# A gated FFN in fp32 split products: two matmuls on the same weight block become one of 512 columns

## The chip, the cores and the metric

The kernel runs on one core of one Trainium2 chip (trn2). The metric is the device time of one execution in microseconds. Engines are named as in the profile: PE is the matmul engine and PEld its weight loads, DVE the vector engine, ACT the scalar engine, POOL the GpSimd engine; SPq and POOLq are the queues on which SyncE and GpSimd start transfers.

## The reference, cut to what matters

One layer of a hybrid block on 512 tokens of width 1024: two token mixers (gated linear attention and a forgetting attention), merged and projected, then a gated MLP of width 2816, then a norm. The change lies in the MLP:

```python
a, val = jnp.split(rmsnorm(x, norm_ffn_g) @ w_up, 2, axis=-1)
a = causal_dwconv(a, conv_w, conv_b)          # width 3, over the tokens
x = x + (jax.nn.gelu(a) * val) @ w_down
```

## The kernel before, in words

Every fp32 product is done as three products of parts: each operand is split into a high part and the rest (`wh`, `wl` of a weight piece, `xh`, `xl` of the activations), and `mm3` issues high-high, high-low and low-high into the same PSUM bank. In the FFN the weight is the stationary operand and the activations are what is streamed: the first matmul is `wh` with `ah`, the second `wh` with `al`, the third `wl` with `ah`, 256 columns each.

The up projection is done by a Strassen-like scheme with seven products instead of eight. The 22 feature tiles are taken as two plain ones (`NCL`) and `NSS` = 10 groups `g` of two. A group has seven products `p`, each with one weight piece of 128 x 1024 (a block of `w_up`, or a sum of blocks) and one operand `xops[p]` (a block of the activations, or a sum). One product is 2 feature tiles x 4 k-steps x 3 matmuls = 24 matmuls. I call the time of one product a slot. `SLOT` gives each product its place within its group; consecutive groups overlap, so that in steady state the order is, by slots of group g: 5(g), 7(g-1), 3(g), 4(g-1), 2(g), 6(g), 1(g+1), and again 5(g+1).

Three PSUM banks belong to a group: `x` gathers products 1 and 2, `z` gathers 5 and 3, `y` gathers 6, 7 and 4. After 1, 5 and 3 `joint` copies the bank to SBUF on ACT (L1461). After 6, DVE adds the copy of 1 onto the bank (L1505) and subtracts into `ap`; after 7 it subtracts again and the convolution follows: two ACT passes (L1393), four DVE multiply-adds (L1397), two Gelus (L1402). After 4 DVE multiplies `x` and `y` by the Gelus (L1520) into `act`, and `sums_of_acts` builds the operands of the down projection.

The weight pieces pass through three buffers (`NW`): `split_next` copies a raw piece to `wh` on ACT (L293) and subtracts to `wl` on DVE (L294), two slots ahead of its product. Behind the split, the `then` lists start what follows: the load of a later piece on SPq (L258), or the addition of a new block onto the raw piece just split, as a transfer with `accum_op=add` on POOLq (L301). These additions turn piece 5 into 6, 3 into 7 and 6 into 4. The piece of product 5 is itself a sum (k12 + k11); for groups 2 to 9 it is formed by `first_sum`: four POOL additions of 256 columns (L264), after the split of piece 2 of the group before.

The order on each engine is chosen by the framework's scheduler from the program order and its own estimates of durations, so it can differ a little from the order of the text.

Of the kernel before, what the change touches and what calls it, by code (L numbers as in the profile page):

```python
# [59 lines left out]
NCL = 2  # L60
NSS = (NF - NCL) // 2

SLOT = {1: -1, 5: 0, 3: 2, 2: 4, 6: 5, 7: 8, 4: 10}

EARLY = (6, 7)

# [24 lines left out]
def hybrid_kernel(ctx: ExitStack, tc, xT, xt, wp, wu, wd, wf, wn, pp, aw2, fing, out):  # L91
# [3 lines left out]
    cpool = ctx.enter_context(tc.tile_pool(name="cpool", bufs=1))  # L95
    wpool = ctx.enter_context(tc.tile_pool(name="wpool", bufs=1))
    banks_of = {}
    es_ps = [None]

    def psum(**tags):  # L100

        if es_ps[0] is not None:
            es_ps[0].close()
        es_ps[0] = ExitStack()
        for tag, bufs in tags.items():
            banks_of[tag] = es_ps[0].enter_context(
                tc.tile_pool(name="ps_" + tag, bufs=bufs, space=PSUM, reuse_waits="tile")
            )

# [6 lines left out]
    def pax():  # L116
        return bank("ax")

    ctx.callback(lambda: es_ps[0].close())
    psum(mm=4, ax=4)  # L120


# [92 lines left out]
    def behind(n, *what):  # L215
        then.setdefault(n, []).append(what)
# [10 lines left out]
    for g in range(NSS):  # L227
        for p, q in ((5, 6), (3, 7), (6, 4)):
            behind(at_step[g, p], "add", at_step[g, q])
        if g + 1 < NSS:  # L230
            if g > 0:
                behind(at_step[g, 2], "first sum", at_step[g + 1, 5], at_step[g + 1, 1])
            behind(at_step[g, 1], "load", at_step[g + 1, 1])
            behind(at_step[g, 2], "load", at_step[g + 1, 2])
        if g + 2 < NSS:
            behind(at_step[g, 7], "load", at_step[g + 2, 5])
            behind(at_step[g, 4], "load", at_step[g + 2, 3])
# [4 lines left out]
    for n, i in zip(freed, at_last):  # L242
        behind(n, "load", i)

    raws, splits, taken, first_copy, after_first, copied, added, last_load = {}, [], [0], [], [], [], [], []
    spare = {}
    rawx_pool, raw_pools = [], {"raw": wpool}

    def load_raw(n):
# [6 lines left out]
            raws[n] = rawx_pool[0].tile([P, 1024], F32, tag=place, name="rawx")  # L256
        for c in (slice(0, WF // 2), slice(WF // 2, WF)) if n == 0 else (slice(0, m),):
            last_load[:] = [nc.sync.dma_start(raws[n][:, c], new[:, c])]  # L258

    def first_sum(n, other, after):  # L260
        for i in range(4):
            c = slice(i * 256, (i + 1) * 256)
            with tc.issue_after(after.ins):
                nc.gpsimd.tensor_add(out=raws[n][:, c], in0=raws[n][:, c], in1=raws[other][:, c])  # L264

    def load_ahead(n):

# [4 lines left out]
    def split_next():  # L272
        n = len(splits)
        if n not in raws:
            load_raw(n)
        raw, m = raws[n], recipes[n][2]
        if n in spare:
            hi, lo = spare[n]()
        else:
            hi = wpool.tile([P, 1024], F32R, tag="wh", name="wh", bufs=NW)  # L280
            lo = wpool.tile([P, 1024], F32R, tag="wl", name="wl", bufs=NW)
        if n < KD:
            if n > 0:
                copied[:] = [nc.scalar.copy(out=hi[:, :WF], in_=raw)]
                copied.append(nc.vector.tensor_sub(out=lo[:, :WF], in0=raw, in1=hi[:, :WF].bitcast(F32)))
            else:
                a, b = slice(0, WF // 2), slice(WF // 2, WF)
                nc.vector.tensor_copy(out=hi[:, a], in_=raw[:, a])
                first_copy.append(nc.vector.tensor_sub(out=lo[:, a], in0=raw[:, a], in1=hi[:, a].bitcast(F32)))
                after_first.append(lambda: nc.scalar.copy(out=hi[:, b], in_=raw[:, b]))  # L290
                after_first.append(lambda: nc.vector.tensor_sub(out=lo[:, b], in0=raw[:, b], in1=hi[:, b].bitcast(F32)))
        else:
            nc.scalar.copy(out=hi[:, :m], in_=raw[:, :m])  # L293
            nc.vector.tensor_sub(out=lo[:, :m], in0=raw[:, :m], in1=hi[:, :m].bitcast(F32))  # L294
        splits.append((hi, lo))
        for what, i, *other in then.get(n, ()):
            if what == "load":
                load_raw(i)
            elif what == "add":
                raws[i] = raw  # L300
                added[:] = [nc.gpsimd.dma_start(raw, recipes[i][0], accum_op=ALU.add)]  # L301
            elif what == "sum":
                dma_behind(lo, raws[i], recipes[other[0]][0], accum_op=ALU.add)
            else:
                first_sum(i, *other, after=added[0])
        for i, b, c in adds_at.get(n, ()):
            dma_behind(lo, wsum[i][:, c], b[:, c], accum_op=ALU.add)

# [133 lines left out]

    xpool = ctx.enter_context(tc.tile_pool(name="xpool", bufs=1))

    xab = [xpool.tile([P, (KD - 2) * T], F32R, name=f"x{c}") for c in "hl"]
    xc = [xpool.tile([P, 1024], F32R, name=f"xc{i}") for i in range(2)]
    xh, xl = (
        [xab[i][:, k * T : (k + 1) * T] for k in range(KD - 2)] + [c[:, i * T : (i + 1) * T] for c in xc]
# [872 lines left out]
    with tc.issue_after(spread_rms(rt, rb).ins):  # L1321
# [8 lines left out]

    KH = KD // 2
    xo = npool.tile([P, 6 * KH * H], F32R, tag="xo", name="xo")
    places2 = [(xo[:, i * 2048 : i * 2048 + 1024], xo[:, i * 2048 + 1024 : (i + 1) * 2048]) for i in range(3)]
    places2 += [tuple(x[:, i * 1024 : (i + 1) * 1024] for x in xab) for i in range(3)] + [tuple(xc)]
    xops = {
        p: tuple(x.rearrange("p (k t) -> p k t", t=H) for x in pl) for p, pl in zip((1, 5, 3, 2, 6, 7, 4), places2)
    }
    x11, x12, x21, x22 = (xs[:, j * KH : (j + 1) * KH, i * H : (i + 1) * H] for i in range(2) for j in range(2))

    def split_x(p, src, after=None):  # L1340
# [63 lines left out]
    def halves(x):  # L1404
        return x.rearrange("p (i t) -> p i t", t=H)
# [40 lines left out]
    def up_product(ps, p, first):  # L1446

        wh, wl = piece()
        ah, al = xops[p]
        for i in range(2):  # L1450
            for k in range(KH):
                c = slice((i * KH + k) * P, (i * KH + k + 1) * P)

                mm3(
                    ps[:, i * H : (i + 1) * H], wh[:, c], wl[:, c], ah[:, k], al[:, k], first and i == k == 0,
                    k == KH - 1, skip_group_check=True,
                )

    def joint(ps):
        x = npool.tile([P, T], F32, tag="joint", name="joint", bufs=4)  # L1460
        nc.scalar.copy(out=x, in_=ps)  # L1461
        return x

    def down(ps, p, piece_no, ws, t2, c0=0, n=512, first=True):

        t = slice(t2 * P, (t2 + 1) * P)
        wh, wl = ws
        ah, al = ops[p % 2]
        for j in range(2):
            k = 2 * piece_no + j  # L1470
            if k == KB:
                break
            c = slice(j * 512 + c0, j * 512 + c0 + n)

            mm3(
                ps[:, c0 : c0 + n], ah[:, k, t], al[:, k, t], wh[:, c], wl[:, c], first and k == 0, k == KB - 1,
                skip_group_check=not first,
            )
# [2 lines left out]

    def first_down(i):
        if not acc1:
            acc1.extend((pax(), pax()))
        ws = piece()
        for t2 in range(2):
            down(acc1[t2], 0, i, ws, t2)

    st_of = {}
    for n, (g, p) in enumerate(steps):  # L1490
        for what in ahead_of.get(n, ()):
            what()
        st = st_of.setdefault(g, {})
        f = NCL + 2 * g
        name = {1: "x", 2: "x", 5: "z", 3: "z", 6: "y", 7: "y", 4: "y"}[p]
        first = name not in st
        if first:

            st[name] = (pax if name == "x" or g == 0 and name == "y" else pmm)()
        ps = st[name]  # L1500
        up_product(ps, p, first)
        if p in (1, 5, 3):
            st[p] = joint(ps)
        elif p == 6:
            nc.vector.tensor_add(out=ps, in0=ps, in1=st[1])  # L1505
            minus_sum(ap[:, :, 2 : H + 2], halves(ps), halves(st[3]))
        elif p == 7:
            minus_sum(ap[:, :, H + 2 : T + 2], halves(ps), halves(st[5]))
            t0 = st["t0"] = npool.tile([P, 2, T], F32, tag="t0", name="t0")
            for i in range(2):  # L1510
                convolve(f + i, i, t0)
        elif p == 4:
            t0 = st["t0"]
            if f // KB == (f + 1) // KB:
                parts = [(f // KB, slice(f % KB, f % KB + 2), slice(0, 2))]
            else:
                parts = [((f + i) // KB, slice((f + i) % KB, (f + i) % KB + 1), slice(i, i + 1)) for i in range(2)]
            for i, c in enumerate((st["x"], ps)):
                for j, k, fs in parts:
                    nc.vector.tensor_mul(  # L1520
                        out=act[j][:, i, k], in0=halves(c)[:, fs], in1=t0[:, fs, i * H : (i + 1) * H]
                    )
            for j, k, _ in parts:
                sums_of_acts(j, k)
        if g == NSS - 1 and p in EARLY:
            first_down(EARLY.index(p))
# [116 lines left out]
    product(2, acc1, first=False)  # L1643
    for t2 in range(2):
        add(acc1[t2], t2, 0, 1)
    acc3 = [pax(), pax()]
    product(3, acc3)
    for t2 in range(2):
        residual(acc3[t2], t2, 0, 512)
# [129 lines left out]
```

## Time and profile before

| | |
|---|---|
| median of 3 runs | 691.87 us (691.44 to 692.91) |
| the profiled execution | 691.86 us |
| its span, first to last instruction | 690.2 us |
| granted TensorE clock | 0.999 |
| busy over the span | PE 683.4, PEld 598.8, DVE 549.3, ACT 426.3, POOL 165.8 us |
| up projection by groups | about 376 to 573 us in the span |
| one period of seven slots in it | 20.16 us |

The shares of busy time say what is full on average; which engine sets the time of a stage is read from the spacing of its instructions and from the waits. A busy matmul is shown longer than the distance to the next one, because matmuls are pipelined; the distance between starts is what one costs in a stream.

### The profile page before, as it was taken

Reading aid. Unit: us, or ns where it says so; the run is one execution under the profiler, and the core shown is the slowest. Engines: PE = TensorE matmul, PEld = TensorE weight load, DVE = VectorE, ACT = ScalarE, POOL = GpSimd, SP = SyncE. Lnnn points to the kernel's source line nnn. Section 1 sums busy time; section 2 is a strip of 40 time slices with the busy share of each in tenths; the row PEclk is TensorE's granted clock in tenths of the full one; section 3 lists DMA queues with packets and bytes.
Section 4 is the critical chain, followed back from the end, with each engine's and each line's share of the span. In section 5 each row is a group of like instructions: output and inputs, shape, how many; then the busy total and the mean of one; then the engine's idle time right before and its main releaser. Section 6 shows DMA issues by size and latency. Waiting matters only on the chain.

```text
span 690.2 us, 11111 instructions
## 1 busy us (share of the span) xinstructions
PE 683.4 (99%) x4131; PEld 598.8 (87%) x4131; DVE 549.3 (80%) x831; ACT 426.3 (62%) x688; POOL 165.8 (24%) x212
## 2 busy tenths in 40 slices
PE   9999999999999999999999999999999999999996
PEld 6788888888888888888888999999999999888886
DVE  6774988858776766677689998888998889977984
ACT  7487676677777744334584866565555557655753
POOL 1125110123321424331110143332434410000222
PEclk9999999999999999999999999999999999999999
DMA  9769488989665489967974877887777788865643
GB/s 312 264 189 305 103 274 218 314 204 207 174 153 118 112 251 212 267 148 218 236 228 119 168 170 188 209 196 164 185 173 175 184 208 255 269 201 175 198 138 122
DMA packets 45034, 138.06 MB, mean 200 GB/s; under 512 B 5268, under 2 KB 9260, under 8 KB 44852
## 3 DMA queue, kind: packets, MB, share of 16 engines
q1 hardware_dynamic: 31156, 92.98, 39.6%
q0 software_dynamic: 10656, 39.33, 32.2%
q10 hardware_dynamic: 3168, 5.05, 2.0%
q8 instruction: 32, 0.52, 0.3%
q14 instruction: 22, 0.18, 0.1%
HBM read 133.13 MB, written 27.28 MB: 232 GB/s over the span
## 4 chain that ended last, share of the span: by engine, by line
PE 96%; DVE 2%; issue 0%; ACT 0%; ACTq 0%
PE ps_mm L330 22%; PE ps_mm L331 22%; PE ps_mm L332 22%; PE ps_ax L332 7%; PE ps_ax L331 7%; PE ps_ax L330 7%; PE ps_lg L1043 1%; PE ps_lg L984 1%; PE ps_pt L1018 1%; PE ps_mm L491 1%; DVE wl L294 1%; PE ps_ax L380 1%; PE ps_ax L887 1%; DVE xo L1344 1%; PE ps_ax L824 0%
## 5 line engine op out<-in xcount | busy, mean ns | idle before, releaser
L293 ACT CAST wh<-rawx 128x1024 fp32r<-128x1024 f32 x75 | 76.1, 1014 | 51.2 <-PE ps_mm L331 18.9
L330 PE MATMUL ps_mm<-xh,wh 128*128 128x512 f32 (+1 forms) x304 | 104.8, 345 | 0.0
L331 PE MATMUL ps_mm<-xl,wh 128*128 128x512 f32 (+1 forms) x304 | 103.2, 340 | 0.0
L332 PE MATMUL ps_mm<-xh,wl 128*128 128x512 f32 (+1 forms) x304 | 103.0, 339 | 0.0
L294 DVE TENSOR_TENSOR wl<-rawx,wh 128x1024 fp32r<-128x1024 f32 x75 | 89.8, 1203 | 14.1 <-ACT wh L293 14.0
L293 ACT CAST wh<-raw 128x1024 fp32r<-128x1024 f32 x58 | 60.6, 1046 | 36.1 <-PE ps_mm L331 30.8
L294 DVE TENSOR_TENSOR wl<-raw,wh 128x1024 fp32r<-128x1024 f32 x58 | 74.3, 1283 | 9.8 <-ACT wh L293 9.6
L330 PEld LDWEIGHTS ps_mm<-xh,wh 128*128 128x128 f32 x304 | 57.7, 190 | 7.6 <-issue 0.9
L332 PEld LDWEIGHTS ps_mm<-xh,wl 128*128 128x128 f32 x304 | 57.7, 190 | 6.5
L331 PEld LDWEIGHTS ps_mm<-xl,wh 128*128 128x128 f32 x304 | 57.7, 190 | 5.9 <-DVE xl L1253 0.2
L301 POOL DMA_DIRECT2D rawx<-in_wu_dram x30 | 26.1, 869 | 117.4 <-DVE wl L294 112.5
L294 DVE TENSOR_TENSOR wl<-rawz,wh 128x1024 fp32r<-128x1024 f32 x31 | 39.4, 1271 | 16.9 <-ACT wh L293 14.9
L264 POOL TENSOR_TENSOR rawx<-rawx,raw 128x256 f32<-128x256 f32 x32 | 39.1, 1250 | 27.2 <-DMA rawx<-in_wu_dram 27.2
L330 PE MATMUL ps_mm<-xo,wh 128*128 128x256 f32 x160 | 45.4, 284 | 0.0
L331 PE MATMUL ps_mm<-xo,wh 128*128 128x256 f32 x160 | 45.3, 283 | 0.0
L332 PE MATMUL ps_mm<-xo,wl 128*128 128x256 f32 x160 | 45.3, 283 | 0.0
L1397 DVE SCALAR_TENSOR_TENSOR t<-ap,ppt,t 128x512 f32<-128x512 f32 x44 | 44.9, 1072 | 0.0
L330 PE MATMUL ps_mm<-xc,wh 128*128 128x256 f32 (+1 forms) x128 | 42.8, 334 | 0.0
L331 PE MATMUL ps_mm<-xc,wh 128*128 128x256 f32 (+1 forms) x128 | 42.3, 330 | 0.0
L332 PE MATMUL ps_mm<-xc,wl 128*128 128x256 f32 (+1 forms) x128 | 42.2, 330 | 0.0
L293 ACT CAST wh<-rawz 128x1024 fp32r<-128x1024 f32 x31 | 32.4, 1044 | 14.1 <-issue 4.9
L330 PE MATMUL ps_mm<-wh,xh 128*128 128x512 f32 x96 | 37.7, 393 | 0.0
(487 smaller groups left out, 1967.4 us busy)
## 6 DMA issues: line engine op xcount, KB each, us to landing
rawx<-in_wu_dram POOLq DMA_DIRECT2D x32, 512.0 KB, 6.5
rawz<-in_wp_dram SPq DMA_DIRECT2D x30, 512.0 KB, 5.3
raw<-in_wp_dram SPq DMA_DIRECT2D x22, 512.0 KB, 4.9
wsum<-in_wd_dram SPq DMA_DIRECT2D x20, 512.0 KB, 6.6
rawx<-in_wu_dram SPq DMA_DIRECT2D x20, 512.0 KB, 6.2
raw<-in_wu_dram SPq DMA_DIRECT2D x20, 512.0 KB, 4.6
rawx<-wsum SPq DMA_DIRECT2D x12, 512.0 KB, 4.5
wsum<-in_wd_dram POOLq DMA_DIRECT2D x10, 512.0 KB, 8.1
```

Of the source, the lines that this page charges most:

```text
L264: nc.gpsimd.tensor_add(out=raws[n][:, c], in0=raws[n][:, c], in1=raws[other][:, c])
L293: nc.scalar.copy(out=hi[:, :m], in_=raw[:, :m])
L294: nc.vector.tensor_sub(out=lo[:, :m], in0=raw[:, :m], in1=hi[:, :m].bitcast(F32))
L301: added[:] = [nc.gpsimd.dma_start(raw, recipes[i][0], accum_op=ALU.add)]
L330: mm(ps, lhsT=ah, rhs=bh, start=start, stop=False, **k)
L331: mm(ps, lhsT=ah, rhs=bl, start=False, stop=False, **k)
L332: mm(ps, lhsT=al, rhs=bh, start=False, stop=stop, **k)
L380: mm(warm, lhsT=nc.const_aps.tensor(1.0, (P, P), BF16), rhs=nc.const_aps.tensor(1.0, (P, T), BF16), start=True, stop=True,)
L491: mm(first[i], lhsT=w[:, i * P : (i + 1) * P], rhs=x, start=(k == j == 0), stop=False)
L887: mm(obs[u][par][:, c], lhsT=scs[2 * u + par][:, 2 * t2 + j, :], rhs=vg[:, 2 * u + t2, h * GDV : (h + 1) * GDV], start=(t2 == j == 0), sto ...
L984: last = mm(lg[:, place_of_q(qb)], lhsT=a[r, q], rhs=b[r, :n], start=(j == 0), stop=(j == 2))
L1397: nc.vector.scalar_tensor_tensor(out=t0[:, i], in0=ap[:, i, w : w + T], scalar=col(C_CW + w * NF + f), in1=t0[:, i], op0=ALU.mult, op1=ALU ...
```

## The change

In groups 2 to 8 (`WIDE`), products 1, 5, 2 and 3 issue two matmuls for each feature tile and k-step instead of three. The first has `wh` as its weights and streams the 256 columns of `ah` and the 256 of `al` as one operand of 512 columns into one whole bank: the left half of the bank gathers high-high, the right half high-low. The second has `wl` and streams `ah` into the left half. So that both parts are reached by one access pattern, `xab` becomes one tile `xw`, and the operands are kept as `both[p]` = [128, 2, k, 256].

A wide tile takes two banks (one for each feature tile), and there are two wide tiles, which replace the four `ax` banks. The two halves are added on the way out: ACT copies the right halves to SBUF, DVE adds them to the left halves. This is done after each of the four products. After 1 the sum goes straight into the bank of `y`, in which 6, 7 and 4 then accumulate, so the DVE addition after 6 goes away in these groups; after 2 the sum goes into `act`, and the multiplication after 4 reads it there instead of in PSUM.

Products 2 and 3 change places in `SLOT`, in all groups. `first_sum` goes away: the sum k12 + k11 for groups 2 to 9 is made by an accumulating transfer on POOLq behind the split of piece 2, with a small POOL copy (`tick`) that holds it back until then. Groups 0, 1 and 9 keep the narrow products, with the evictions moved in the same way.

```diff
+WIDE = range(2, NSS - 1)
-SLOT = {1: -1, 5: 0, 3: 2, 2: 4, 6: 5, 7: 8, 4: 10}
+SLOT = {1: -1, 5: 0, 2: 2, 3: 4, 6: 5, 7: 8, 4: 10}
...
-                behind(at_step[g, 2], "first sum", at_step[g + 1, 5], at_step[g + 1, 1])
+                behind(at_step[g, 2], "sum", at_step[g + 1, 5], at_step[g + 1, 1])
...
-    def first_sum(n, other, after):
-        for i in range(4):
-            c = slice(i * 256, (i + 1) * 256)
-            with tc.issue_after(after.ins):
-                nc.gpsimd.tensor_add(out=raws[n][:, c], in0=raws[n][:, c], in1=raws[other][:, c])
...
-    xab = [xpool.tile([P, (KD - 2) * T], F32R, name=f"x{c}") for c in "hl"]
+    xw = xpool.tile([P, 2, (KD - 2) * T], F32R, name="xw")
+    xab = [xw[:, i] for i in range(2)]
...
+    def wide_product(ps, p, first):
+
+        wh, wl = piece()
+        for i in range(2):
+            for k in range(KH):
+                c = slice((i * KH + k) * P, (i * KH + k + 1) * P)
+                mm(ps[:, i], lhsT=wh[:, c], rhs=both[p][:, :, k], start=first and k == 0, stop=False, skip_group_check=True)
+                mm(
+                    ps[:, i, 0], lhsT=wl[:, c], rhs=both[p][:, 0, k], start=False, stop=k == KH - 1,
+                    skip_group_check=True,
+                )
+
+    def joint(g, ps, out=None, tag="joint3"):
+
+        if out is None or g in WIDE:
+            x = npool.tile([P, 2, H], F32, tag=tag, name=tag, bufs=2)
+            out = out or [(x, slice(0, 2))]
+        if g in WIDE:
+            nc.scalar.copy(out=x, in_=ps[:, :, 1])
+        for o, c in out:
+            if g in WIDE:
+                nc.vector.tensor_add(out=o, in0=ps[:, c, 0], in1=x[:, c])
+            else:
+                nc.scalar.copy(out=o, in_=halves(ps)[:, c])
+        return out[0][0]
...
+    psum(keep=1, wide=2)
...
-        up_product(ps, p, first)
-        if p in (1, 5, 3):
-            st[p] = joint(ps)
+        (wide_product if name != "y" and g in WIDE else up_product)(ps, p, first)
+        if p == 1 and g < WIDE[0]:
+            st[1] = joint(g, ps, [(act[1][:, 1, KB - 2 * g - 2 : KB - 2 * g], slice(0, 2))])
+        elif p == 1:
+            st["y"] = pmm()
+            joint(g, ps, [(halves(st["y"]), slice(0, 2))])
+        elif p == 2:
+            joint(g, ps, [(act[j][:, 0, k], fs) for j, k, fs in parts_of(f)])
+        elif p in (3, 5):
+            st[p] = joint(g, ps, tag=f"joint{p}")
         elif p == 6:
-            nc.vector.tensor_add(out=ps, in0=ps, in1=st[1])
-            minus_sum(ap[:, :, 2 : H + 2], halves(ps), halves(st[3]))
+            if g < WIDE[0]:
+                nc.vector.tensor_add(out=halves(ps), in0=halves(ps), in1=st[1])
+            minus_sum(ap[:, :, 2 : H + 2], halves(ps), st[3])
```

More of the change, by code (lines that the diff above doesn't have):

```diff
@@ L97, in hybrid_kernel, with psum @@
     banks_of = {}
[L98 to L104, printed above, removed]
+    es_ps = []
+    def psum(keep=0, **tags):
+        while len(es_ps) > keep:
+            es_ps.pop().close()
         for tag, bufs in tags.items():
-            banks_of[tag] = es_ps[0].enter_context(
+            es_ps.append(ExitStack())
+            banks_of[tag] = es_ps[-1].enter_context(
                 tc.tile_pool(name="ps_" + tag, bufs=bufs, space=PSUM, reuse_waits="tile")
@@ L117, in pax, with pwide @@
         return bank("ax")
-    ctx.callback(lambda: es_ps[0].close())
+    def pwide():
+        return banks_of["wide"].tile([P, 2, 512], F32, tag="wide", name="ps_wide")
+    ctx.callback(psum)
     psum(mm=4, ax=4)
@@ L243, in hybrid_kernel @@
         behind(n, "load", i)
-    raws, splits, taken, first_copy, after_first, copied, added, last_load = {}, [], [0], [], [], [], [], []
+    raws, splits, taken, first_copy, after_first, copied, last_load = {}, [], [0], [], [], [], []
     spare = {}
@@ L300, in split_next @@
                 raws[i] = raw
-                added[:] = [nc.gpsimd.dma_start(raw, recipes[i][0], accum_op=ALU.add)]
-            elif what == "sum":
+                nc.gpsimd.dma_start(raw, recipes[i][0], accum_op=ALU.add)
+            else:
                 dma_behind(lo, raws[i], recipes[other[0]][0], accum_op=ALU.add)
-            else:
-                first_sum(i, *other, after=added[0])
         for i, b, c in adds_at.get(n, ()):
@@ L1332, in hybrid_kernel @@
     xo = npool.tile([P, 6 * KH * H], F32R, tag="xo", name="xo")
[L1333 to L1337, printed above, removed]
+    places2 = [xo[:, i * 2048 : (i + 1) * 2048].rearrange("p (a n) -> p a n", a=2) for i in range(3)]
+    places2 += [xw[:, :, i * 1024 : (i + 1) * 1024] for i in range(3)]
+    both = {p: x.rearrange("p a (k t) -> p a k t", t=H) for p, x in zip((1, 5, 3, 2, 6, 7), places2)}
+    xops = {p: (x[:, 0], x[:, 1]) for p, x in both.items()}
+    xops[4] = tuple(x.rearrange("p (k t) -> p k t", t=H) for x in xc)
     x11, x12, x21, x22 = (xs[:, j * KH : (j + 1) * KH, i * H : (i + 1) * H] for i in range(2) for j in range(2))
@@ L1457, in up_product @@
                 )
[L1459 to L1462, printed above, removed]
+    def wide_product(ps, p, first):
[17 more added lines that the diff above has]
+                nc.vector.tensor_add(out=o, in0=ps[:, c, 0], in1=x[:, c])
+            else:
+                nc.scalar.copy(out=o, in_=halves(ps)[:, c])
+        return out[0][0]
     def down(ps, p, piece_no, ws, t2, c0=0, n=512, first=True):
@@ L1483, in first_down @@
         if not acc1:
-            acc1.extend((pax(), pax()))
+            acc = pwide()
+            acc1.extend(acc[:, t2] for t2 in range(2))
         ws = piece()
@@ L1487, in first_down, with parts_of @@
             down(acc1[t2], 0, i, ws, t2)
+    psum(keep=1, wide=2)
+    def parts_of(f):
+        if f // KB == (f + 1) // KB:
+            return [(f // KB, slice(f % KB, f % KB + 2), slice(0, 2))]
+        return [((f + i) // KB, slice((f + i) % KB, (f + i) % KB + 1), slice(i, i + 1)) for i in range(2)]
     st_of = {}
@@ L1497, in hybrid_kernel @@
         if first:
-            st[name] = (pax if name == "x" or g == 0 and name == "y" else pmm)()
-        ps = st[name]
-        up_product(ps, p, first)
-        if p in (1, 5, 3):
-            st[p] = joint(ps)
+            if name == "y":
+                st[name] = pmm()
+            elif g in WIDE:
+                st[name] = pwide().rearrange("p i (a t) -> p i a t", t=H)
+            else:
+                st[name] = pwide()[:, 0]
+        ps = st[name]
+        (wide_product if name != "y" and g in WIDE else up_product)(ps, p, first)
[8 more added lines that the diff above has]
+            st[p] = joint(g, ps, tag=f"joint{p}")
         elif p == 6:
-            nc.vector.tensor_add(out=ps, in0=ps, in1=st[1])
-            minus_sum(ap[:, :, 2 : H + 2], halves(ps), halves(st[3]))
+            if g < WIDE[0]:
+                nc.vector.tensor_add(out=halves(ps), in0=halves(ps), in1=st[1])
+            minus_sum(ap[:, :, 2 : H + 2], halves(ps), st[3])
         elif p == 7:
-            minus_sum(ap[:, :, H + 2 : T + 2], halves(ps), halves(st[5]))
+            minus_sum(ap[:, :, H + 2 : T + 2], halves(ps), st[5])
             t0 = st["t0"] = npool.tile([P, 2, T], F32, tag="t0", name="t0")
@@ L1513, in hybrid_kernel @@
             t0 = st["t0"]
[L1514 to L1519, printed above, removed]
+            for i in range(2):
+                for j, k, fs in parts_of(f):
+                    a = act[j][:, i, k]
                     nc.vector.tensor_mul(
-                        out=act[j][:, i, k], in0=halves(c)[:, fs], in1=t0[:, fs, i * H : (i + 1) * H]
+                        out=a, in0=a if i == 0 else halves(ps)[:, fs], in1=t0[:, fs, i * H : (i + 1) * H]
                     )
-            for j, k, _ in parts:
+            for j, k, _ in parts_of(f):
                 sums_of_acts(j, k)
@@ L1645, in hybrid_kernel @@
         add(acc1[t2], t2, 0, 1)
-    acc3 = [pax(), pax()]
+    acc = pwide()
+    acc3 = [acc[:, t2] for t2 in range(2)]
     product(3, acc3)
```

## The prediction, made before the changed kernel ran

> **What bounds the kernel now.** I read the page first, then the busy time by windows of one group period, then the distances between matmul starts, then each queue of one period.
>
> ```profile
> span 690.2 us, 11111 instructions
> PE 683.4 (99%) x4131; PEld 598.8 (87%) x4131; DVE 549.3 (80%) x831; ACT 426.3 (62%) x688; POOL 165.8 (24%) x212
> ...
> PE 96%; DVE 2%; issue 0%; ACT 0%; ACTq 0%
> ```
>
> The third line is the chain of work that ended last: 96% of it is PE. The next view is busy time by stretches of 20.16 us, one period of seven products (columns: PE, PEld, DVE, ACT, POOL, granted clock, DMA share, GB/s; the sum is over eight such stretches).
>
> ```profile
> 404.12:424.28 20.16, 20.16 (x170) 20.16 (x169) 18.10 (x21) 11.90 (x16) 7.21 (x8) 1.00 0.76 168
> 444.44:464.60 20.16, 20.16 (x170) 20.16 (x169) 17.20 (x19) 11.90 (x16) 7.58 (x8) 1.00 0.75 182
> 525.08:545.24 20.16, 20.16 (x170) 20.16 (x169) 17.80 (x19) 11.38 (x15) 8.02 (x9) 1.00 0.75 176
> sum 161.28, PE 161.28 PEld 161.28 DVE 140.45 ACT 93.41 POOL 57.53; mean PE 20.16 PEld 20.16 DVE 17.56 ACT 11.68 POOL 7.19
> ```
>
> PE has no gap, DVE is at 17.56 of 20.16 (87%), DMA at about 0.76. So in this stage a matmul less is time less, as long as nothing else reaches the period. What a matmul costs is the distance between starts. In the timeline of PE, the first of these rows and the last are 35 matmuls apart:
>
> ```profile
> 449.73 0.28 PE L330 MATMUL ps_mm<-xh,wh 128*128 128x256 f32 x1
> ...
> 453.93 0.28 PE L332 MATMUL ps_ax<-xo,wl 128*128 128x256 f32 x1
> ```
>
> (453.93 - 449.73) / 35 = 0.120 us for 256 columns; 168 of them are 20.16 us, the whole period. The 512-column matmuls of the down projection, 35 from the first to the second row below, and the two places where the width changes:
>
> ```profile
> 585.83 0.39 PE L330 MATMUL ps_ax<-wh,acth 128*128 128x512 f32 x1
> ...
> 593.76 0.39 PE L332 MATMUL ps_ax<-wh,actl 128*128 128x512 f32 x1
> ...
> 669.92 0.39 PE L332 MATMUL ps_ax<-wh,actl 128*128 128x512 f32 x1
> 670.15 0.28 PE L330 MATMUL ps_ax<-wh,acth 128*128 128x256 f32 x1
> 670.26 0.28 PE L331 MATMUL ps_ax<-wl,acth 128*128 128x256 f32 x1
> ...
> 671.58 0.40 PE L330 MATMUL ps_ax<-wh,acth 128*128 128x512 f32 x1
> 671.81 0.40 PE L331 MATMUL ps_ax<-wl,acth 128*128 128x512 f32 x1
> 672.05 0.39 PE L332 MATMUL ps_ax<-wh,actl 128*128 128x512 f32 x1
> 672.28 0.40 PE L330 MATMUL ps_ax<-wh,acth 128*128 128x512 f32 x1
> ```
>
> (593.76 - 585.83) / 35 = 0.2266 us. Doubling the columns adds 0.1066 us, so 0.0134 us of every matmul does not depend on its width.
>
> **The change, part by part.**
>
> *Matmuls.* Products 1, 5, 2, 3 in 7 groups, 8 pairs of feature tile and k-step each: 4 x 7 x 8 = 224 times, two matmuls of 0.120 become one of 0.2266: 0.0134 us saved, 3.0 us in all. The columns streamed stay the same; what goes is one start and one weight load. The unknowns are alternation and the access pattern. Narrow and wide now take turns; just after narrow ones, a 512 took (672.28 - 671.58) / 3 = 0.2333, which would halve the gain to 0.0067 each, 1.5 us; just after a wide one a 256 took 0.11, which speaks for the full gain. I take 0.0134, with 1.5 us as the low end. The wide operand is two runs of 256 columns apart in SBUF; no row before has that, and its bound is rival B.
>
> A page of the Trainium skill speaks against the 3.0. "TensorE: Matmul & The Clock Gate", section "Back-to-back issue gap", gives a gap of N / 2.4 + 2.5 ns at full clock, so a fixed part of 2.5 ns, by which 224 merges are worth about 0.6 us (an estimate). The rows here differ (13.4 ns beyond the same slope), and I go by the rows.
>
> *Evictions, DVE and ACT.* In each wide group DVE gains an addition after 1, 5, 3 and 2 and loses that after 6: three more. Each has one PSUM and one SBUF input, like L1505 (columns: busy us, mean ns):
>
> ```profile
> L1505 DVE TENSOR_TENSOR ps_mm<-ps_mm,joint 128x512 f32<-128x512 f32 x8 | 5.5, 689 | 0.0
> ```
>
> 3 x 0.69 = 2.1 us more per group. Against it stands what the POOL additions cost DVE today. The convolution's four multiply-adds in a group while POOL adds (422.8 to 427.5), and in the last group, where it does not (563 to 567):
>
> ```profile
> L1397 DVE SCALAR_TENSOR_TENSOR t<-ap,ppt,t 128x512 f32<-128x512 f32 x4 | 4.7, 1226 | 0.0
> ...
> L1397 DVE SCALAR_TENSOR_TENSOR t<-ap,ppt,t 128x512 f32<-128x512 f32 x4 | 2.7, 743 | 0.0
> ```
>
> With `first_sum` gone, 4 x (1.226 - 0.743) = 1.9 us per group come back. Net DVE is 17.56 + 2.1 - 1.9 = 17.8 of a new period of 20.16 - 32 x 0.0134 = 19.73 us (90%): hidden behind PE, cost 0. ACT gains one copy of the left-over half per group (0.58 us as the present `joint` copies have it, 11.7 to 12.3 of 19.73): 0. The place where DVE is latest is behind the convolution:
>
> ```profile
> 443.03 4.68 DVE L1397 SCALAR_TENSOR_TENSOR t<-ap,ppt,t 128x512 f32<-128x512 f32 x4
> 447.63 1.21 DVE L294 TENSOR_TENSOR wl<-rawx,wh 128x1024 fp32r<-128x1024 f32 x1
> ```
>
> This `wl` ends at 448.84 and its product begins at 449.37: 0.5 us to spare. Afterwards the convolution is 1.9 us shorter and one addition (after 2) comes in front: about 1.7 us to spare. If that cover were gone, lateness past 0.5 us would be PE time, rival C.
>
> *PSUM.* `x` and `z` rotate through two wide tiles. The next group's 5 needs `z` back two slots (5.6 us) after 3 ends; a copy (0.58) and an addition (0.69) fit. Cost 0; the exchange of 2 and 3 leaves 3 directly before 6, whose subtraction waits for the addition, still on DVE alone.
>
> *The sum of pieces as a transfer.* Per group, four POOL additions go; a `tick` copy, a POOLq issue (0.86 us) and 512 KB of accumulating DMA come, all for groups 2 to 9. Rows for 384 to 570 us (packets, MB, share of 16 engines; then count, size, us from issue to landing):
>
> ```profile
> q0 software_dynamic: 4035, 14.68, 48.7%
> q1 hardware_dynamic: 5328, 19.40, 28.3%
> ...
> rawx<-in_wu_dram POOLq DMA_DIRECT2D x28, 512.0 KB, 6.5
> ```
>
> One accumulation takes 0.487 x 186 / 28 = 3.2 us of all sixteen engines. The DMA share goes from 0.76 x 20.16 = 15.3 to 18.5 of 19.73 us, 94%: nearly full, not over. So its chain has to be followed:
>
> ```profile
> 456.01 0.33 SPq L258 DMA_DIRECT2D rawx<-in_wu_dram  x1
> 462.33 4.98 POOL L264 TENSOR_TENSOR rawx<-rawx,raw 128x256 f32<-128x256 f32 x4 [3.66 <-DMA rawx<-in_wu_dram]
> 450.00 1.04 ACT L293 CAST wh<-rawx 128x1024 fp32r<-128x1024 f32 x1
> 452.30 1.22 DVE L294 TENSOR_TENSOR wl<-rawx,wh 128x1024 fp32r<-128x1024 f32 x1
> ```
>
> The block of a later product 5 is loaded at 456.01 and landed at 462.33, when POOL began. As a transfer from there, the sum lands at 462.33 + 6.5 = 468.8. The cast of that piece comes one period after the one at 450.00, at 470.2 (469.7 with the shorter period): 0.9 us to spare, and PE itself needs it only at 475.29 - 0.43, less 1.05 and 1.22 for cast and subtraction, 472.6: 3.8 us. Queued behind it on POOLq is 3 into 7, whose own split now comes at about 463.3 because 3 is a slot pair later; it waits about an engine's 3.2 us behind the sum, landing near 473, for a cast due at 472.5 and a product at 478: hidden as well. The loads on SPq are four per group as before, with 2's and 3's exchanged. Cost 0.
>
> *The start of the stage.* The exchange of 2 and 3 also concerns group 0, where DVE is the late one:
>
> ```profile
> 382.78 0.28 PE L331 MATMUL ps_ax<-xl,wh 128*128 128x256 f32 x1
> 383.15 0.39 PE L332 MATMUL ps_ax<-xh,wl 128*128 128x256 f32 x1
> ...
> 381.88 1.21 DVE L294 TENSOR_TENSOR wl<-raw,wh 128x1024 fp32r<-128x1024 f32 x1
> ```
>
> PE waited 0.37 - 0.12 = 0.25 us there for 2's `wl`. Product 2 now is due in full before 3; either its split moves ahead of another and the 0.25 goes, or it stays behind and up to one more DVE step (1.2 us) shows. I take +0.2, nearer the present row since the same total work is due one slot later; ends -0.25 and +1.2. Down projection: the same matmuls in other banks, 0.
>
> **Sum** against the profiled execution, 691.86 us (the median is 691.87, so the same): 691.86 - 3.0 + 0.2 = 689.1 us.
>
> **The rivals.** Less than 0.2% (1.4 us) either way I call no change; a measurement of this kernel tells no more.
>
> A, the forecast: 689.1, its own range 688.6 (full gain, the present wait gone) to 690.5 (half the gain and 0.2 lost).
>
> B, the change doesn't do what it says: the fixed part is paid for each run of the operand, so a wide matmul costs 2 x 0.120. For it: no row shows a two-run operand. Against: the fixed part is the same at 256 and 512 columns, so it goes with the instruction. Time 691.86 + 0.2 = 692.1. By the page of the Trainium skill named above it would be about 691.5 (an estimate: 691.86 - 0.6 + 0.2).
>
> C, DVE becomes the bound in part: the convolution stays long, because POOL's transfers disturb it, and the additions stand in its way: 17.56 + 2.1 = 19.7 of 19.73 us, no slack. Against it is the short convolution of the last group, which had POOL transfers around it. If each wide group then loses 0.3 us (an addition of 0.69 plus the lost 0.1 of slack, less the 0.5 to spare): 7 x 0.3 = 2.1, 691.2.
>
> D, slower: the sum lands too late for product 5. It decides once it lands after 472.6, by the times above. That happens if the scheduler puts 3 into 7 ahead of the sum on POOLq: issued at 463.5, the sum at 464.4, landing at 464.4 + 6.5 + 3.2 = 474.1, 1.5 us late. A stall gives the next group's chain its time back, so it is paid about every other of eight groups: 4 x 1.5 = 6, 695.1 us. For it: DMA at 94%. Against: the sum stands first in the text, and its transfer is ready a microsecond earlier.
>
> **How the numbers follow.** A 0.70, B 0.08, C 0.12, D 0.10. B and C end within 0.2%: faster 0.70, same 0.20, slower 0.10. The range runs from A's low end, 688.6, less 0.1 for rounding, to 691.6, which takes in C and the half gain with the worst start (691.86 - 1.5 + 1.2); outside it are B, D and little else.
>
> **What would show it.** Right: in the wide groups starts 0.227 and 0.120 apart in turn and a period of 19.73 us with no PE gap; L1397 at 0.74 us in all groups; DMA at 0.94. Wrong: starts of 0.24 (B); `wl` ending after its product's slot begins, with PE waiting on DVE behind a convolution (C); a cast waiting for the accumulating transfer before product 5 (D); a PE gap near 383 above 1 us.

## The result, and the profile after

The changed kernel takes 697.51 us (median of 4 runs, 697.1 to 698.3) against 691.71 us for the kernel before on the same chip: ratio 1.0082, 95% interval 1.0064 to 1.0099. It is 5.8 us slower; 3.0 us faster in the matmuls and 689.1 us in all were forecast. The profiled execution took 697.54 us. All medians in this document are of executions at a granted clock of 0.99 or more; of the kernel with adjacent halves, below, one of 8 executions ran at 0.752 and is left out.

The top of the page and the chain:

```profile
span 695.8 us, 10697 instructions
PE 683.5 (98%) x3907; PEld 588.4 (85%) x3907; DVE 546.3 (79%) x852; ACT 432.1 (62%) x698; POOL 137.0 (20%) x196
...
PE 97%; ACT 1%; DVE 1%; issue 0%; DVEq 0%; ACTq 0%
```

The span is 5.6 us longer with 224 matmuls fewer, and PE's busy time has not fallen. Two periods of the wide groups, each stretch from the first matmul of a product 3 to that of the next group's:

```profile
433.26:453.20 19.94, 19.94 (x139) 18.45 (x137) 17.02 (x22) 12.55 (x17) 3.64 (x5) 1.00 0.93 213
453.20:473.13 19.93, 19.93 (x138) 18.44 (x137) 17.01 (x23) 12.53 (x17) 3.64 (x5) 1.00 0.93 211
```

In the changed groups PE has no gap and the period fell from 20.16 to 19.93 us: that part is faster, by half of what was forecast. The loss is elsewhere. Stretches of 4 us at the start of the stage (columns as before: PE, PEld, DVE, ACT, POOL, granted clock, DMA share, GB/s):

```profile
380.00:384.00 4.00, 2.60 (x21) 2.40 (x21) 4.00 (x5) 3.61 (x6) 0.86 (x1) 1.00 0.90 214
384.00:388.00 4.00, 4.00 (x36) 4.00 (x35) 3.54 (x6) 3.97 (x5) 0.86 (x1) 1.00 0.89 168
388.00:392.00 4.00, 4.00 (x36) 4.00 (x35) 4.00 (x5) 2.92 (x4) 0.00 (x0) 1.00 1.03 207
392.00:396.00 4.00, 0.44 (x4) 0.23 (x2) 4.00 (x5) 1.08 (x2) 0.86 (x1) 0.79 0.69 135
396.00:400.00 4.00, 3.40 (x16) 3.40 (x17) 3.02 (x5) 1.55 (x3) 0.00 (x0) 0.50 0.62 185
400.00:404.00 4.00, 4.00 (x29) 3.85 (x29) 1.23 (x1) 1.53 (x2) 0.00 (x0) 0.86 0.00 0
```

PE stands still at 382 and at 392, and behind the second gap it runs at a granted clock of 0.50. None of these groups has a wide matmul. The PE timeline at the two gaps, with what released it in brackets:

```profile
381.86 0.28 PE L328 MATMUL ps_wide<-xo,wl 128*128 128x256 f32 x1
383.54 0.39 PE L326 MATMUL ps_wide<-xo,wh 128*128 128x256 f32 x1 [1.40 <-ACT joint L1479]
...
392.16 0.28 PE L328 MATMUL ps_wide<-xo,wl 128*128 128x256 f32 x1
396.60 0.58 PE L326 MATMUL ps_wide<-xw,wh 128*128 128x256 f32 x1 [4.17 <-ACT act L1479]
396.98 0.41 PE L327 MATMUL ps_wide<-xw,wh 128*128 128x256 f32 x1
397.20 0.41 PE L328 MATMUL ps_wide<-xw,wl 128*128 128x256 f32 x1
...
401.04 0.33 PE L328 MATMUL ps_wide<-xw,wl 128*128 128x256 f32 x1
```

Beyond the usual 0.12 us the gaps are 1.56 and 4.32 us. From 396.60 to 401.04 run 20 matmuls of 256 columns, 0.222 us apart instead of 0.120: 2.0 us more. Together that is 7.9 us. Less the 0.25 us that the kernel before lost here, and less the 7 x 0.23 = 1.6 us that the wide groups gain, 6.0 us are left, against the 5.8 us measured. The last matmul before the long gap belongs to product 1 of group 1, the first after it to product 2 of group 0, which waits for a copy of ACT into `act`. What that copy waited for, in the timelines of ACT and DVE:

```profile
395.97 1.07 ACT L1479 COPY act<-ps_wide 128x512 f32<-128x512 f32 x2 [2.52 <-DVE xc L1341]
...
394.72 1.21 DVE L1341 TENSOR_TENSOR xc<-xs,xc 128x1024 fp32r<-128x1024 f32 x1
```

These are the copies of product 1 for groups 0 and 1. In both, the change writes them not into a `joint` tile but into an unused part of `act[1]`; so the description above, by which these groups have their evictions moved in the same way as the wide ones, passes over a difference. That tile is `block("act2", 2, x2pool)`, and `xs`, the activations, has the same tag `act2` in the same pool with one buffer: tiles with one tag share that buffer in turn, so they are the same memory. The copy can't start before the last reader of `xs`, the split of x22 for product 4 (`xc<-xs`), has ended at 395.9. Until the copy is done the bank `x` of group 0 is not free, product 2 can't accumulate in it, and the scheduler put product 2 behind products 3 and 6 of group 0 and 1 of group 1.

### The profile page after: what moved, and what is told of

It reads as the page before. It is cut to its first block, busy times and chain, and to the rows that moved or that the text cites. A ratio compares the mean times of both kernels' runs of the same rounds, so it can differ in the third digit from the quotient of the medians.

```text
span 695.8 us, 10697 instructions
## 1 busy us (share of the span) xinstructions
PE 683.5 (98%) x3907; PEld 588.4 (85%) x3907; DVE 546.3 (79%) x852; ACT 432.1 (62%) x698; POOL 137.0 (20%) x196
## 4 chain that ended last, share of the span: by engine, by line
PE 97%; ACT 1%; DVE 1%; issue 0%; DVEq 0%; ACTq 0%
PE ps_mm L326 20%; PE ps_mm L328 20%; PE ps_mm L327 20%; PE ps_wide L1462 8%; PE ps_wide L326 5%; PE ps_wide L327 5%; PE ps_wide L328 5%; PE ps_wide L1463 4%; PE ps_lg L1040 1%; PE ps_lg L981 1%; PE ps_pt L1015 1%; PE ps_mm L488 1%; PE ps_ax L326 1%; PE ps_ax L327 1%; PE ps_ax L328 1%; PE ps_ax L376 1%
## 5 line engine op out<-in xcount | busy, mean ns | idle before, releaser
L326 PE MATMUL ps_mm<-xw,wh 128*128 128x512 f32 (+1 forms) x320 | 109.3, 341 | 0.0
L327 PE MATMUL ps_mm<-xw,wh 128*128 128x512 f32 (+1 forms) x320 | 107.8, 337 | 0.0
L328 PE MATMUL ps_mm<-xw,wl 128*128 128x512 f32 (+1 forms) x320 | 107.6, 337 | 0.0
L326 PEld LDWEIGHTS ps_mm<-xw,wh 128*128 128x128 f32 x320 | 60.5, 189 | 8.2 <-issue 0.9
L328 PEld LDWEIGHTS ps_mm<-xw,wl 128*128 128x128 f32 x320 | 60.5, 189 | 6.4
L327 PEld LDWEIGHTS ps_mm<-xw,wh 128*128 128x128 f32 x320 | 60.6, 189 | 5.9 <-DVE xw L1250 0.2
L1462 PE MATMUL ps_wide<-xo,wh 128*128 128x512 f32 x168 | 60.0, 399 | 0.0
L1463 PE MATMUL ps_wide<-xo,wl 128*128 128x256 f32 x168 | 47.2, 281 | 0.0
L307 POOL COPY tick<-wl 128x1 f32<-128x1 f32 x37 | 10.9, 295 | 136.1 <-DVE wl L292 136.1
L1462 PEld LDWEIGHTS ps_wide<-xo,wh 128*128 128x128 f32 x168 | 31.6, 188 | 7.2
L326 PE MATMUL ps_mm<-wh,xw 128*128 128x512 f32 x96 | 37.7, 393 | 0.0
L327 PE MATMUL ps_mm<-wl,xw 128*128 128x512 f32 x96 | 37.4, 390 | 0.0
```

Source lines behind the costliest of these rows:

```text
L307: now = nc.gpsimd.tensor_copy(out=tick, in_=lo[:, 0:1].bitcast(F32))
L326: mm(ps, lhsT=ah, rhs=bh, start=start, stop=False, **k)
L327: mm(ps, lhsT=ah, rhs=bl, start=False, stop=False, **k)
L328: mm(ps, lhsT=al, rhs=bh, start=False, stop=stop, **k)
L1462: mm(ps[:, i], lhsT=wh[:, c], rhs=both[p][:, :, k], start=first and k == 0, stop=False, skip_group_check=True)
L1463: mm(ps[:, i, 0], lhsT=wl[:, c], rhs=both[p][:, 0, k], start=False, stop=k == KH - 1, skip_group_check=True,)
```

## The experiments

Each is a change to the changed kernel unless said otherwise; the medians are of the runs on one chip with the kernel before beside them.

**Product 1's copy in its own tile.** Theory 1 is the shared memory. Theory 2 is that the exchange of 2 and 3 is at fault, which the prediction had priced at most at 1.2 us.

```diff
-            st[1] = joint(g, ps, [(act[1][:, 1, KB - 2 * g - 2 : KB - 2 * g], slice(0, 2))])
+            st[1] = joint(g, ps)
```

> The changed kernel, with product 1 of groups 0 and 1 copied into an ordinary joint tile instead of into act2. Theory 1 (act2 shares its memory with the activations xs, so the copy must wait for the last reader of xs, and product 2 waits for the copy): the two PE gaps of 1.56 and 4.32 us at 382 and 392 us go, and with them the half-speed matmuls behind the second (about 2.2 us); the time is 697.5 - 8.1 + up to 0.5 = 689.4 to 690.0 us. Theory 2 (the exchange of products 2 and 3 makes product 2 due before its operands are ready): the gaps stay, 697 us. The wide groups keep their period of 19.93 us by both.

690.06 us (10 runs, 689.3 to 691.27) against 691.76: ratio 0.9976, interval 0.9967 to 0.9986. No gap over 0.08 us is left between 370 and 600 us. The ACT timeline shows the copy of product 1 where it was in the kernel before, at 380 instead of 396 (the first row is from the kernel before, the others are from this one):

```profile
380.05 0.57 ACT L1461 COPY joint<-ps_ax 128x512 f32<-128x512 f32 x1
...
379.16 1.04 ACT L1339 CAST xw<-xs 128x1024 fp32r<-128x1024 f32 x1
380.11 0.57 ACT L1479 COPY joint<-ps_wide 128x512 f32<-128x512 f32 x1
380.59 1.05 ACT L291 CAST wh<-rawx 128x1024 fp32r<-128x1024 f32 x1
```

One line moves the change from 0.8% slower to 0.24% faster. Theory 1 is borne out; the 7.5 us between the two medians are the 7.9 us above, but for 0.4.

**The same line alone, in the kernel before.**

```diff
+    def joint_act(g, ps):
+        o = act[1][:, 1, KB - 2 * g - 2 : KB - 2 * g]
+        nc.scalar.copy(out=o, in_=halves(ps))
+        return o
...
-            st[p] = joint(ps)
+            st[p] = joint_act(g, ps) if p == 1 and g < 2 else joint(ps)
...
```

The addition after 6 takes the shape of that copy.

> The kernel before, with one thing of the change alone: product 1 of groups 0 and 1 is copied into act2 instead of into a joint tile. Theory 1: product 2 of group 0 has to wait for the split of x22, a PE gap of 3 to 5 us near 390 to 396 us and slow matmuls behind it, 691.7 + 4 to 8 = 696 to 700 us. Theory 2: no gap, 691.7 us.

694.77 us (4 runs, 694.71 to 694.82): ratio 1.0043, interval 1.0028 to 1.0058. Both gaps appear in the old order, with narrow products only:

```profile
382.54 0.28 PE L332 MATMUL ps_mm<-xo,wl 128*128 128x256 f32 x1
384.23 0.39 PE L330 MATMUL ps_mm<-xo,wh 128*128 128x256 f32 x1 [1.41 <-ACT joint L1461]
...
395.73 0.28 PE L332 MATMUL ps_mm<-xo,wl 128*128 128x256 f32 x1
397.51 0.39 PE L330 MATMUL ps_ax<-xh,wh 128*128 128x256 f32 x1 [1.50 <-ACT act L1466]
397.73 0.28 PE L331 MATMUL ps_ax<-xl,wh 128*128 128x256 f32 x1
397.85 0.28 PE L332 MATMUL ps_ax<-xh,wl 128*128 128x256 f32 x1
```

So the first gap, too, comes from this line: with product 2 blocked nothing was there to run while product 3 waited for the copy of 5. I had expected 4 to 8 us; it is 3.0, because the second gap is 1.66 us here and the clock stays up behind it (0.12 us at 397.73). A gap of 4.3 us cost the clock, one of 1.7 did not. The Trainium skill, "TensorE: Matmul & The Clock Gate", section "What's actually happening", has the clock fall to half after an idle window of about 3.4 us; these two gaps lie on either side of it, and the granted 0.50 is its half.

**The old order, with the copy still in the shared memory.**

```diff
-SLOT = {1: -1, 5: 0, 2: 2, 3: 4, 6: 5, 7: 8, 4: 10}
+SLOT = {1: -1, 5: 0, 3: 2, 2: 4, 6: 5, 7: 8, 4: 10}
```

> The changed kernel with products 3 and 2 in their old places (3 before 2), and product 1 of groups 0 and 1 still copied into act2. Theory 1: product 2 still waits for the same split, so a PE gap stays; as 2 is due a slot pair later the gap is smaller by what runs before it, 694 to 698 us. Theory 2: the gaps go, 690.2 us.

699.58 us (4 runs, 699.42 to 700.22), ratio 1.0115, interval 1.01 to 1.013. The gaps at the start stay (1.56 and 4.23 us), so the exchange isn't their cause; my forecast that the second would shrink was wrong. And every wide group gets a small gap, of about 0.27 us, which the next experiment shows without the late start.

**The old order, with the copy in its own tile.** The edits of the first and the third experiment.

> e1_joint with products 3 and 2 in their old places. If the exchange of 2 and 3 is needed in steady state (in e3_old_order each wide group showed a PE gap of about 0.27 us in which product 5 waited for the DVE addition of product 3 to free its bank): 7 x 0.27 = 1.9 us over e1_joint, about 692 us. If those gaps came from the late start of e3_old_order: the time of e1_joint within 0.3 us, 690 us.

692.84 us (10 runs, 692.12 to 693.67), ratio 1.0012, interval 1.0003 to 1.0022: 2.8 us over the first experiment. Each wide group loses about 0.27 us at the start of product 3; the timelines of PE and of its weight loads at that place, in two groups:

```profile
440.38 0.28 PE L328 MATMUL ps_mm<-xw,wl 128*128 128x256 f32 x1
440.66 0.50 PE L1462 MATMUL ps_wide<-xo,wh 128*128 128x512 f32 x1
441.00 0.28 PE L1463 MATMUL ps_wide<-xo,wl 128*128 128x256 f32 x1
...
440.66 0.19 PEld L1462 LDWEIGHTS ps_wide<-xo,wh 128*128 128x128 f32 x1 [0.21 <-DVE joint L1477]
...
460.59 0.28 PE L328 MATMUL ps_mm<-xw,wl 128*128 128x256 f32 x1
460.87 0.50 PE L1462 MATMUL ps_wide<-xo,wh 128*128 128x512 f32 x1
```

The period, from 440.66 to 460.87, is 20.21 us. I had named the wait the wrong way round: it is product 3 that waits for the addition after 5 to free their bank `z`. In the old order one product lies between 5 and 3, in the new one three, and that is what the exchange is worth; 7 x 0.27 = 1.9 of the 2.8 us are these gaps. Another 0.5 us is lost between 382.6 and 383.8, where product 2 of group 0 waits for its `wl` as in the kernel before (0.25) and two more matmuls start 0.1 late; the first experiment's kernel has none of this. The rest I have not placed.

**Why a pair costs more than 0.347 us.** By the uniform rows of the kernel before, a wide and a narrow matmul would take 0.2266 + 0.120 = 0.347 us. In the changed kernel, one wide product from its first matmul to the next product's first:

```profile
453.20 0.40 PE L1462 MATMUL ps_wide<-xo,wh 128*128 128x512 f32 x1
453.43 0.28 PE L1463 MATMUL ps_wide<-xo,wl 128*128 128x256 f32 x1
453.55 0.40 PE L1462 MATMUL ps_wide<-xo,wh 128*128 128x512 f32 x1
...
456.03 0.28 PE L326 MATMUL ps_mm<-xw,wh 128*128 128x256 f32 x1
```

(456.03 - 453.20) / 8 = 0.354 us a pair, 0.006 under three narrow ones. The rows put 0.23 on the wide matmul and 0.12 on the narrow one. Theory 3: the two runs of the operand. Theory 4: the change of width.

```diff
-    places2 = [xo[:, i * 2048 : (i + 1) * 2048].rearrange("p (a n) -> p a n", a=2) for i in range(3)]
+    places2 = [xo[:, i * 2048 : (i + 1) * 2048].rearrange("p (k a t) -> p a k t", a=2, t=H) for i in range(3)]
...
```

> e1_joint with the operands of products 1, 5 and 3 laid out so that for each k-step the 256 high and the 256 low columns are adjacent: their wide matmul streams one run of 512. Product 2 keeps its two runs. Theory 3 (the pair costs 0.353 us instead of 0.347 because the operand has two runs): pairs of products 1, 5, 3 take 0.347, those of 2 take 0.353, and the time is 168 x 0.0067 = 1.1 us under e1_joint. Theory 4 (a 512-column matmul after a 256-column one costs 0.233, whatever its operand): all pairs take 0.353 and the time is that of e1_joint within 0.3 us.

689.72 us (7 runs, 689.57 to 690.54), ratio 0.9973, interval 0.9962 to 0.9984: no different from the first experiment. Its pairs are read from the same kernel, run once more:

> The kernel of e4_adjacent once more, since its profile fell into an execution at a lower granted clock (0.752) and its pairs can't be read: operands of products 1, 5, 3 with high and low adjacent, product 2 with two runs. Theory 3 (two runs cost): pairs 0.347 us in products 1, 5, 3, 0.353 in 2, 1.1 us under e1_joint. Theory 4 (a 512 behind a 256 costs 0.233): 0.353 in all, the time of e1_joint within 0.3 us.

690.09 us (5 runs, 689.42 to 690.46), ratio 0.9967, interval 0.9954 to 0.998. A product with adjacent halves:

```profile
445.39 0.40 PE L1462 MATMUL ps_wide<-xo,wh 128*128 128x512 f32 x1
445.62 0.28 PE L1463 MATMUL ps_wide<-xo,wl 128*128 128x256 f32 x1
...
448.22 0.28 PE L326 MATMUL ps_mm<-xw,wh 128*128 128x256 f32 x1
```

(448.22 - 445.39) / 8 = 0.354 us. The two runs cost nothing; theory 3 falls, and with it rival B of the prediction.

**Eight wide matmuls, then eight narrow ones**, in the loops of `wide_product`:

```diff
                 mm(ps[:, i], lhsT=wh[:, c], rhs=both[p][:, :, k], start=first and k == 0, stop=False, skip_group_check=True)
+        for i in range(2):
+            for k in range(KH):
+                c = slice((i * KH + k) * P, (i * KH + k + 1) * P)
                 mm(
                     ps[:, i, 0], lhsT=wl[:, c], rhs=both[p][:, 0, k], start=False, stop=k == KH - 1,
...
```

> e1_joint with the eight wide matmuls of a product first and its eight narrow ones behind them, operands in two runs as in the change. Theory 4 (the extra 0.0067 us goes with the change of width): 512-column matmuls go down to 0.227 us after the first few of a run (about six took 0.233 in the kernel before), so a product takes 2.77 to 2.82 us instead of 2.83 and the time is 0 to 1.5 us under e1_joint. Theory 3 (two runs cost): all wide ones stay at 0.233, and the time is that of e1_joint.

689.97 us (5 runs, 689.59 to 690.96), ratio 0.997, interval 0.9957 to 0.9983. Merged rows of one product:

```profile
479.46 2.00 PE L1462 MATMUL ps_wide<-xw,wh 128*128 128x512 f32 x8
481.30 1.12 PE L1466 MATMUL ps_wide<-xw,wl 128*128 128x256 f32 x8
482.26 0.28 PE L326 MATMUL ps_mm<-xc,wh 128*128 128x256 f32 x1
```

1.84 us for eight wide ones is 0.230 each. This product takes 2.80 us, and a group, from product 4 to product 4, 19.81 us (442.63 to 462.44) instead of 19.94 (442.81 to 462.75 in the first experiment's kernel): 7 x 0.13 = 0.9 us by the rows, in line with theory 4; the medians (0.1 us apart) can't show it. With both edits:

> e4_adjacent and e5_runs together: in products 1, 5, 3 one run of 512 columns, eight wide matmuls in a row; in product 2 two runs, eight in a row. Theory 3: 0.227 throughout in products 1, 5, 3, and 0.233 in 2. Theory 4: the same course in all four products, 0.233 first and 0.227 later; the time of e5_runs within 0.3 us.

689.07 us (4 runs, 688.75 to 689.6), ratio 0.9954, interval 0.9939 to 0.9968: the fastest kernel of the study, 0.9 us under the one before, where theory 4 gave at most 0.3. Its wide products have the same 1.84 us for eight, so the adjacency adds nothing there; its stage merely begins 0.6 us earlier than that of the one before, which I can't explain and don't count.

**The sums for product 5 on POOL again.** `first_sum` and its entry in `then` are put back into the first experiment's kernel.

> e1_joint with the sums for product 5 made on POOL again (four additions of 256 columns) instead of by an accumulating transfer. If the transfer is what pays for the added DVE additions, as the prediction reckoned: the four multiply-adds of the convolution are back at 1.2 us, DVE rises to about 19.0 of 19.93 us, the weight splits behind the convolution come late, and the time is 0.5 to 2.5 us over e1_joint. If DVE has slack without it: the multiply-adds take 1.2 us all the same, but PE shows no gap and the time is that of e1_joint within 0.3 us. The DMA share goes from 0.91 back to about 0.77 by both.

691.43 us (10 runs, 690.53 to 692.93), ratio 0.9994, interval 0.9984 to 1.0003: 1.4 us over the first experiment, the lower half of what the first theory gave. The rows answer as reckoned (windows, then the DVE group of the convolution):

```profile
431.50:451.50 20.00, 20.00 (x138) 18.46 (x137) 18.78 (x22) 12.71 (x17) 7.58 (x7) 1.00 0.73 183
...
L1402 DVE SCALAR_TENSOR_TENSOR t<-ap,ppt,t 128x512 f32<-128x512 f32 x24 | 27.1, 1186 | 0.0
...
491.82 0.39 PE L1471 MATMUL ps_wide<-xo,wl 128*128 128x256 f32 x1 [0.35 <-DVE wl L298]
```

DVE is at 18.8 us in a stretch of 20.0, and PE waits now and then for a weight split; from the product 4 that starts at 422.14 to the one seven groups on, at 563.12, a group takes 20.14 us; between the same two products of the first experiment's kernel (422.88 and 562.59) it takes 19.96. This is rival C, brought about by putting the POOL additions back.

**No wide group at all.**

```diff
-WIDE = range(2, NSS - 1)
+WIDE = range(NSS, NSS + 1)
```

> e1_joint with no wide group: all products issue three matmuls of 256 columns; the new order, banks, evictions of product 2 and the accumulating transfers stay. If the merge alone gives the gain, at 0.0067 us for each of 224: 690.1 + 1.5 = 691.6 us, a period of 20.16 us. If the rest of the change gives part of it: under 691 us.

691.71 us (10 runs, 691.17 to 692.02), ratio 0.9995, interval 0.9986 to 1.0005, with a period of 20.16 us:

```profile
431.66:451.82 20.16, 20.16 (x170) 20.16 (x169) 15.44 (x18) 12.39 (x16) 3.63 (x5) 1.00 0.93 213
```

The merge is worth 691.71 - 690.06 = 1.65 us, and 7 x 0.23 = 1.6 by the periods. The new banks, the order, the move of product 2 into `act` and the transfers together neither cost nor gain. The extra additions of the wide groups aren't in this kernel, so their price is within the 1.65; PE has no gap in the wide groups that would speak for one.

## Why the prediction was wrong, point by point

*Evictions* is the step that failed. It went through the additions and copies of the wide groups and gave them the cost 0, which is right. It left out where the narrow groups put theirs: for groups 0 and 1 the diff names `act[1]` as the destination of product 1's copy, and I did not ask what else lives there. A destination is a wait like any other. `act2` is shared with `xs`, and the copy was moved from 380 to 396 us; it cost 7.5 us, by the first experiment. The time came out slower, as only rival D had it, but not in D's way.

*The start of the stage* was considered, but for the wrong thing. I followed the weight split of product 2 (0.25 us, up to 1.2), which was not late. The condition in the prediction's own list, a PE gap near 383 above 1 us, did come: 1.56 us, with a larger one behind it. With the copy in its own tile the exchange even removes the 0.25 us wait (no gap over 0.08 us is left there), so the term was -0.25, its low end, and not +0.2.

*Matmuls*: the merge did save time, but half as much as forecast. I took 0.0134 us for each merge, the value of a long row of 512s, over 0.0067, the value just behind a change of width, though in the new stream every wide matmul stands behind a narrow one. Measured are 0.006 to 0.007 (period 20.16 to 19.93 us, 0.23 over 32 merges) and 1.65 us in all, by the kernel without wide groups. The nearest row was the one at 671.58, and I had it. That 0.0134 us goes with the instruction whatever its width was no finding either: two spacings always give one slope and one remainder. The Trainium skill, "TensorE: Matmul & The Clock Gate", section "Back-to-back issue gap", gives its fixed part of 2.5 ns for a single matmul; with it the merges would have been worth about 0.6 us (an estimate). The measured 1.65 lies between that and the 3.0 forecast.

*DVE*: 17.8 us per group forecast, 17.0 measured. The convolution came down to its 0.74 us in all groups:

```profile
L1394 DVE SCALAR_TENSOR_TENSOR t<-ap,ppt,t 128x512 f32<-128x512 f32 x8 | 5.5, 744 | 0.0
```

The trade of POOL additions against DVE additions was read rightly, and the kernel with POOL sums shows its price without it: 1.4 us, where C had 2.1. That C's 691.2 us is so near to the 691.4 measured is luck, since C took the full gain of the merge.

*The sum as a transfer*: DMA at 0.93 against 0.94 forecast, and no PE gap ahead of product 5 in the wide groups; D did not occur. *PSUM*: the wide tiles cost nothing, but only with the exchange of 2 and 3; in the old order the addition after product 5 holds the bank that 3 wants, 0.27 us per group. I had followed `z` only from 3 to the next 5.

With the copy in its own tile, the 690.06 us lie inside the forecast's own range of 688.6 to 690.5, but 1 us above its 689.1: the merge gave half of what was taken.

## What to carry to other kernels

Ask of each new destination in a diff which tile's memory it is and who reads that memory last; a scratch area that looks free by its index can be a wait on another engine's whole queue. Where a gain rests on a spacing, take it from the row with the same neighbours as the new stream, not from the longest uniform row. And a loss in a stage that the change's name does not mention is found by setting the windows of the whole stage side by side, before any thought about the mechanism that was changed.

## What the runs showed of the hardware that I had not expected

A 512-column matmul takes 0.2266 us in a long row of its kind and 0.230 on average in rows of eight; in turn with a 256-column one the two take 0.354, where 0.2266 and 0.120 would make 0.347; the layout of its operand in one run or two made no difference (0.354 us a pair in both). Why the change of width costs this is open: no run here tells a cause apart. The DVE multiply-adds of the convolution, with both tensors in SBUF, took 0.74 us each, and about 1.2 us beside POOL additions, in the kernels that have them. An idle gap of PE of 4.3 us brought the granted clock to 0.50 for the next 20 matmuls; gaps of 1.56 and 1.66 us did not.
